# Gate/up projections of four feed-forward blocks by one level of Strassen

## The chip, the cores and the metric

The kernel runs on one core of a Trainium2 chip. The metric is the device time of one execution in microseconds (us). The engines are named as the profile names them: PE is TensorE (PEld its weight loads), DVE VectorE, ACT ScalarE, POOL GpSimd, and SP the engine that here only asks for transfers.

## The reference

A decoder trunk of two layers on 512 tokens of 1024 features, in float32. Each layer is a half-step feed-forward block (FFN), a mixer, and another half-step FFN; layer 0 mixes by attention, layer 1 by an S5 state space.

```python
def swiglu(h, w_gate, w_up, w_down):
    return (jax.nn.silu(h @ w_gate) * (h @ w_up)) @ w_down

for i in range(DEPTH):                       # DEPTH = 2
    x = x + 0.5 * swiglu(rmsnorm(x, ffn1_norm[i]), ffn1_gate[i], ffn1_up[i], ffn1_down[i])
    h = rmsnorm(x, mix_norm[i])
    x = x + mixer(h)                         # attention for i = 0, S5 for i = 1
    x = x + 0.5 * swiglu(rmsnorm(x, ffn2_norm[i]), ffn2_gate[i], ffn2_up[i], ffn2_down[i])
```

The hidden width is 2816, 22 tiles of 128. So there are four FFNs, FFN0 to FFN3, with attention after FFN0 and S5 after FFN2.

## The kernel before

The state `x` lies in SBUF with the features on the partitions: 8 feature tiles of 128 x 512 tokens. Every float32 product is made of three float32r passes (`mm3`, L135 to L139): each operand is split into a high part, rounded to float32r, and a low part, the rest; high x high, high x low and low x high are added up in PSUM.

Weights come through the class `Stream` in the order in which PE reads them: 1 MB loads on SP (L49), up to four in SBUF, the high part by an ACT cast (`wh`, L77) and the low part by a DVE subtraction (`wl`, L79), for 1024 columns at a time and up to three such splits ahead. `ahead` runs after each matmul group.

An FFN goes through its 22 hidden tiles. For each it has two groups of 24 matmuls of 128x128 weights by 512 tokens (`ps_gu`: gate, then up); `post` (L269 to L280) then scales both by `R` (1/rms of each token), takes the swish of the gate on ACT (L272), multiplies (L275) and splits the product into `ah` (ACT, L277) and `al` (DVE, L279). After 6, 12, 17 and 22 tiles the down projection of those tiles follows, for 8 output tiles (`ps_d`), and `upd` (L315) adds half of it to `x`. At the last of them `nxt(d)` starts the next stage's operands for feature tile `d`: `norm_split` makes `xh` on ACT (L195) and `xl` on DVE (L196), and `norm_sum` adds the squares (L203 to L208).

Tables for attention and S5 are made beside the FFNs as background work: `tick(k, rate)` takes steps of generators in `k.bg` after each matmul group until they have used about `rate` microseconds of DVE, by a formula in `Counted`; the rate is 2.0 in FFN0 and 1.4 in FFN1 and FFN2. Every engine takes its instructions in the order written; nothing reorders them.

Of the kernel before, what the change touches and what calls it, by code (L numbers as in the profile page):

```python
# [15 lines left out]
P = 128  # L16
W = 516                                  # columns of a shared working tile
GROUPS = [(0, 6), (6, 6), (12, 5), (17, 5)]
HALF_PI = (1.5703125, 4.837512969970703125e-4, 7.549789948768648e-8)
LN2 = (0.693359375, -2.12194440e-4)  # L20
MAGIC = 12582912.0                       # 1.5 * 2**23: rounds to an integer when added


class Stream:
    """Weights in the order the tensor engine reads them: 1 MB loads, then the exact
    split into a float32r high part (ScalarE) and low part (VectorE)."""

    RAW = 4

    def __init__(self, nc, raw, hl, ahead_load=3, ahead_split=3):  # L30
        self.nc, self.raw, self.hl = nc, raw, hl
        self.AL, self.AS = ahead_load, ahead_split
        self.units, self.gr = [], []
        self.nl = self.ns = self.cur = self.done = 0
        self.rt, self.wt = {}, {}

    def add(self, ap, ncols, grs, split=True):
        u = len(self.units)
        self.units.append((ap, ncols))
        for a, b in grs:  # L40
            self.gr.append((u, a, b, split))

    def load(self, pieces=((0, 2048),)):
        ap, n = self.units[self.nl]
        t = self.raw.tile([P, 2048], F32, tag="raw", name="raw")
        self.rt[self.nl] = t
        self.nl += 1
        for a, b in pieces:
            self.nc.sync.dma_start(t[:, a:min(b, n)], ap[:, a:min(b, n)])  # L49
            yield  # L50

    def load_to(self, u, force=False):
        while self.nl <= min(u, len(self.units) - 1):
            if not force and self.nl - self.RAW >= self.done:
                break
            for _ in self.load():
                pass

    def split_to(self, g, pieces=None, later=None):
        while self.ns <= min(g, len(self.gr) - 1):  # L60
            u, a, b, sp = self.gr[self.ns]
            self.load_to(u, True)
            r = self.rt[u]
            if sp == "pairs":
                h = self.hl.tile([P, 1024], F32R, tag="wh", name="wh")
                z = h[:, :2 * (b - a)].rearrange("p (k two c) -> p k two c", two=2, c=8)
                v = r[:, a:b].rearrange("p (k c) -> p k c", c=8)
                self.nc.scalar.copy(z[:, :, 0], v)
                self.nc.vector.tensor_tensor(z[:, :, 1], v, z[:, :, 0].bitcast(F32), ALU.subtract)
                self.wt[self.ns] = (h, None)  # L70
                self.done = u + 1
            elif sp:
                h = self.hl.tile([P, 1024], F32R, tag="wh", name="wh")
                lo = self.hl.tile([P, 1024], F32R, tag="wl", name="wl")
                for c0, c1 in pieces or ((0, b - a),):
                    rest = (lo[:, c0:c1], r[:, a + c0:a + c1], h[:, c0:c1].bitcast(F32), ALU.subtract)
                    self.nc.scalar.copy(h[:, c0:c1], r[:, a + c0:a + c1])  # L77
                    if later is None:
                        self.nc.vector.tensor_tensor(*rest)  # L79
                    else:  # L80
                        later.append(rest)
                self.wt[self.ns] = (h, lo)
                if self.ns + 1 == len(self.gr) or self.gr[self.ns + 1][0] != u:
                    self.done = u + 1
            else:
                self.wt[self.ns] = (r[:, a:b], None)
            self.ns += 1

    def next(self):
        g = self.cur  # L90
        self.cur += 1
        if g and not self.gr[g - 1][3]:
            self.done = self.gr[g - 1][0] + 1
        self.split_to(g)
        return self.wt.pop(g)

    def finish(self):
        """the units taken so far are read by no later instruction"""
        self.done = self.gr[self.cur - 1][0] + 1

    def ahead(self, later=None):
        """the next splits and loads; VectorE's half of the splits is left to the caller if asked"""
        g = self.cur
        if g < len(self.gr):
            e = min(g + self.AS, len(self.gr) - 1)
            while not self.gr[e][3] and e > g:
                e -= 1
            if self.gr[e][3]:
                self.split_to(e, later=later)
            self.load_to(self.gr[e][0] + self.AL)  # L110


class Counted:
    """VectorE calls of background work, with their length added up."""
# [20 lines left out]
def mm3(nc, ps, wh, wl, xh, xl, start, stop):  # L135
    """one float32 block product in three float32r passes"""
# [5 lines left out]
def rsqrt_steps(k, V, v, n, scale, eps):  # L142
    """v [P, n] sums; yields between steps, last the tile with 1/sqrt(v*scale + eps)"""
# [28 lines left out]
def tick(k, us):  # L172
    """background work worth about `us` of VectorE"""
# [14 lines left out]
# ---------------------------------------------------------------- norms  # L188
def norm_split(k, d, ni):
    """the split of x*g of a feature tile"""  # L190
    if d == 0:
        k.xh = k.big.tile([P, 8, 512], F32R, tag="big", name="xh")
        k.xl = k.big.tile([P, 8, 512], F32R, tag="big", name="xl")
# [4 lines left out]

def norm_sum(k, d):
    """sums of squares"""  # L200
# [28 lines left out]
def stats2(k):  # L229
    """the same, [128 equal rows, 512 tokens]"""  # L230
# [7 lines left out]
# ---------------------------------------------------------------- feed-forward  # L238
def ffn_order():
    o, done = [], 0  # L240
    for gi, (s, n) in enumerate(GROUPS):
        upto = s + n + (0 if gi == len(GROUPS) - 1 else 1)
        while done < upto:
            o.append(("gu", done))
            done += 1
        o.append(("d", gi))
    return o


def ffn_units(st, wgu, wd6, wd5):  # L250
    for kind, i in ffn_order():
        if kind == "gu":
            st.add(wgu[i], 2048, [(0, 1024), (1024, 2048)])
        else:
            n = GROUPS[i][1]
            for j in range(4):
                ap = wd6[i * 4 + j] if i < 2 else wd5[(i - 2) * 4 + j]
                st.add(ap, 2 * n * 128, [(0, n * 128), (n * 128, 2 * n * 128)])


def ffn(k, nxt, rate=0.0, sums=None):
# [3 lines left out]
    act = {}  # L265
    wait = []

    def post():
        m, gp, up = wait.pop(0)  # L269
        g1 = k.G("g1")[:, :512]  # L270
        V.tensor_tensor(g1, gp, k.R, ALU.mult)  # L271
        S.activation(g1, g1, AF.Silu)  # L272
        u1 = k.G("u1")[:, :512]
        V.tensor_tensor(u1, up, k.R, ALU.mult)  # L274
        V.tensor_tensor(u1, g1, u1, ALU.mult)  # L275
        ah = k.G("ah", F32R)[:, :512]
        S.copy(ah, u1)  # L277
        al = k.G("al", F32R)[:, :512]
        V.tensor_tensor(al, u1, ah.bitcast(F32), ALU.subtract)  # L279
        act[m] = (ah, al)  # L280

    for kind, i in ffn_order():
        if kind == "gu":
            ps = []
            for h in range(2):
                w, lo = st.next()
                p = k.PS("ps_gu")
                for kk in range(8):
                    c = slice(kk * 128, kk * 128 + 128)
                    mm3(nc, p, w[:, c], lo[:, c], k.xh[:, kk], k.xl[:, kk], kk == 0, kk == 7)  # L290
                ps.append(p)
                st.ahead()
                if sums and st.AS == 2:
                    run_out(sums)
                    st.AS = 3
                g = 2 * i + h - (1 if sums else 0)
                if g == 1:
                    stats1(k)
                elif g == 2:
                    stats2(k)  # L300
# [1351 lines left out]
```

## Time and profile before

| | |
|---|---|
| Time, median of 3 runs | 1940.06 us (1938.75 to 1940.76) |
| Span of the profiled execution | 1938.9 us |
| Stages: start 0 to 20; FFN0 to 420; attention to 640; FFN1 to 1020; FFN2 to 1400; S5 to 1560; FFN3 to the end | us, rounded |

The span is that of one profiled execution, and everything below is read from it; it lies 1.2 us under the median. A busy share counts the time that an engine works on instructions. Matmuls are pipelined: each is shown longer (0.39 us) than the distance from one start to the next, which is what one costs. "Idle before" and "waits" name the instruction that let a waiting engine go on.

### The profile page before, as it was taken

The numbers are of one execution on the slowest core, as the hardware profiler recorded it, in microseconds if no ns is written. First come the engines' busy times: TensorE is split into PE (matmuls) and PEld (weight loads), VectorE is DVE, ScalarE is ACT, GpSimd is POOL, SyncE is SP. The second block draws the span as 40 slices with busy tenths as digits, with TensorE's granted clock in tenths as the row PEclk, the third lists the DMA queues.
The fourth block names the chain that finished last, engine by engine and source line by source line (L and its number), as shares of the span: only waits on it lengthen the run. The fifth ranks groups of instructions, "written<-read, shape, count | busy, mean of one in ns | idle before, by whom it ended". The sixth has DMA issues, their size and how long they took to land.

```text
span 1938.9 us, 22606 instructions
## 1 busy us (share of the span) xinstructions
PE 1927.5 (99%) x8740; PEld 1560.2 (80%) x8740; DVE 1129.0 (58%) x2153; ACT 672.4 (35%) x1104; POOL 100.6 (5%) x183
## 2 busy tenths in 40 slices
PE   9999999999999999999999999999999999999999
PEld 6788888877788888888888888888888888888887
DVE  6787676557685665456457556444484644444443
ACT  5222222434557432322324322322463432222221
POOL 0000111000011000100100100100000000000000
PEclk9999999999999999999999999999999999999999
DMA  6222334234122323433423443433486322222221
GB/s 246 102 103 97 127 106 134 88 109 125 52 84 56 118 88 125 152 101 108 171 93 129 132 141 104 143 124 106 154 260 208 131 95 80 103 88 97 71 98 44
DMA packets 62780, 227.40 MB, mean 117 GB/s; under 512 B 23744, under 2 KB 23872, under 8 KB 46672
## 3 DMA queue, kind: packets, MB, share of 16 engines
q1 hardware_dynamic: 42736, 192.47, 28.9%
q0 software_dynamic: 11472, 31.36, 5.3%
q10 hardware_dynamic: 8464, 2.12, 0.5%
q8 instruction: 69, 1.13, 0.2%
q14 instruction: 39, 0.32, 0.1%
HBM read 196.17 MB, written 26.61 MB: 115 GB/s over the span
## 4 chain that ended last, share of the span: by engine, by line
PE 96%; DMA 1%; ACT 1%; DVE 1%; issue 1%; SPq 0%; DVEq 0%; ACTq 0%
PE ps_gu L137 17%; PE ps_gu L139 17%; PE ps_gu L138 17%; PE ps_d L138 8%; PE ps_d L139 8%; PE ps_d L137 8%; PE ps_p L421 2%; PE ps_p L423 2%; PE ps_p L422 2%; PE ps_g L137 2%; PE ps_g L138 2%; PE ps_g L139 2%; PE ps_s L1173 1%; PE ps_w L137 1%; PE ps_w L138 1%; PE ps_w L139 1%
## 5 line engine op out<-in xcount | busy, mean ns | idle before, releaser
L137 PE MATMUL ps_gu<-xh,wh 128*128 128x512 f32 x1408 | 561.4, 399 | 2.8 <-ACT xh L195 2.8
L139 PE MATMUL ps_gu<-xh,wl 128*128 128x512 f32 x1408 | 557.7, 396 | 0.0
L138 PE MATMUL ps_gu<-xl,wh 128*128 128x512 f32 x1408 | 555.9, 395 | 0.2 <-DVE xl L196 0.2
L77 ACT CAST wh<-raw 128x1024 fp32r<-128x1024 f32 (+3 forms) x354 | 334.1, 947 | 518.6 <-PE ps_d L138 250.4
L79 DVE TENSOR_TENSOR wl<-raw,wh 128x1024 fp32r<-128x1024 f32 (+3 forms) x235 | 260.3, 1110 | 174.4 <-ACT wh L77 172.7
L137 PEld LDWEIGHTS ps_gu<-xh,wh 128*128 128x128 f32 x1408 | 265.0, 188 | 66.7 <-ACT xh L195 3.1
L139 PEld LDWEIGHTS ps_gu<-xh,wl 128*128 128x128 f32 x1408 | 264.9, 188 | 65.2
L138 PEld LDWEIGHTS ps_gu<-xl,wh 128*128 128x128 f32 x1408 | 265.0, 188 | 64.5 <-DVE xl L196 1.1
L137 PE MATMUL ps_d<-ah,wh 128*128 128x512 f32 x704 | 277.9, 395 | 0.0
L138 PE MATMUL ps_d<-al,wh 128*128 128x512 f32 x704 | 277.4, 394 | 0.0
L139 PE MATMUL ps_d<-ah,wl 128*128 128x512 f32 x704 | 277.3, 394 | 0.0
L315 DVE SCALAR_TENSOR_TENSOR x<-ps_d,x 128x512 f32<-128x512 f32 x128 | 88.5, 691 | 193.0 <-PE ps_d L139 192.7
L274 DVE TENSOR_TENSOR u<-ps_gu,R 128x512 f32<-128x512 f32 x88 | 60.8, 691 | 194.7 <-PE ps_gu L139 194.7
L137 PEld LDWEIGHTS ps_d<-ah,wh 128*128 128x128 f32 x704 | 132.2, 188 | 30.8
L139 PEld LDWEIGHTS ps_d<-ah,wl 128*128 128x128 f32 x704 | 132.2, 188 | 30.8
L138 PEld LDWEIGHTS ps_d<-al,wh 128*128 128x128 f32 x704 | 132.3, 188 | 30.6
L277 ACT CAST ah<-u 128x512 fp32r<-128x512 f32 x88 | 54.7, 622 | 267.4 <-DVE u L275 265.0
L272 ACT ACTIVATE g<-g 128x512 f32<-128x512 f32 x88 | 55.7, 633 | 206.4 <-DVE g L271 206.4
L318 DVE TENSOR_TENSOR wl<-raw,wh 128x1024 fp32r<-128x1024 f32 (+2 forms) x101 | 104.7, 1036 | 0.3 <-ACT wh L77 0.3
L279 DVE TENSOR_TENSOR al<-u,ah 128x512 fp32r<-128x512 f32 x88 | 61.0, 693 | 60.5 <-ACT ah L277 60.5
L421 PE MATMUL ps_p<-wh,xh 128*128 128x512 f32 x192 | 79.0, 411 | 0.0
L423 PE MATMUL ps_p<-wh,xl 128*128 128x512 f32 x192 | 76.0, 396 | 0.0
(298 smaller groups left out, 1939.1 us busy)
## 6 DMA issues: line engine op xcount, KB each, us to landing
raw<-in_wgu SPq DMA_DIRECT2D x87, 1024.0 KB, 4.8
raw<-in_wd SPq DMA_DIRECT2D x32, 768.0 KB, 4.4
raw<-in_wd SPq DMA_DIRECT2D x32, 640.0 KB, 3.9
raw<-in_wq SPq DMA_DIRECT2D x12, 1024.0 KB, 4.8
raw<-in_wglu SPq DMA_DIRECT2D x8, 1024.0 KB, 4.9
raw<-in_wo SPq DMA_DIRECT2D x4, 1024.0 KB, 4.8
dW<-t POOLq DMA_DIRECT2D x16, 256.0 KB, 2.5
dY<-y POOLq DMA_DIRECT2D x16, 256.0 KB, 3.3
```

Source lines behind the costliest of these rows:

```text
L77: self.nc.scalar.copy(h[:, c0:c1], r[:, a + c0:a + c1])
L79: self.nc.vector.tensor_tensor(*rest)
L137: nc.tensor.matmul(ps, wh, xh, start=start, stop=False)
L138: nc.tensor.matmul(ps, wh, xl, start=False, stop=False)
L139: nc.tensor.matmul(ps, wl, xh, start=False, stop=stop)
L272: S.activation(g1, g1, AF.Silu)
L274: V.tensor_tensor(u1, up, k.R, ALU.mult)
L279: V.tensor_tensor(al, u1, ah.bitcast(F32), ALU.subtract)
L315: V.scalar_tensor_tensor(k.x[:, d], p, 0.5, k.x[:, d], ALU.mult, ALU.add)
L318: V.tensor_tensor(*a)
L421: T.matmul(ps[t], xh, w[:, c], start=kk == 0, stop=False)
L423: T.matmul(ps[t], xl, w[:, c], start=False, stop=kk == 7)
```

## The change

Gate and up projections are done for pairs of hidden tiles (`NPAIR = 11` per FFN). The weights of a pair are cut in four by the halves of the hidden tile pair and of the features (a11, a12, a21, a22), the normalised input in four by features and tokens. One level of Strassen's method makes the product of two such 2x2 arrangements from seven half-size products, P1 to P7, instead of eight, with sums of weight blocks, sums of input blocks and sums of results.

- **Products.** `prod` issues 24 matmuls of 256 tokens: 4 pairs of feature tiles x gate and up x 3 passes. `ffn_plan` sets the order P1, P4 of the pair before, P2, P5, P6, P3, P7. The first pair of an FFN interleaves P1, P2 and P5 (`first`). Down projections follow every second pair, with three pairs in the last group. The down projection's matmuls are the same in number and size.
- **Weight sums.** Units are of 512 KB, up to eight in SBUF. P5 needs a21 + a22 and P7 needs a11 + a21: the second block is added to the first while it is loaded, by a DMA on the POOL queue (`flush`). For P6 and P3 DVE adds another unit to P5's (`then`). Seven splits of 1024 columns per pair replace four, up to two ahead.
- **Input sums.** `forms` makes the seven sums of input blocks for each pair of feature tiles and splits each into `Fh` and `Fl`; for FFN0 its additions are on POOL, elsewhere on DVE.
- **Result sums.** P1, P5 and the sum called U2 are copied from PSUM by ACT (`hold`); c11, c12, c21 and c22 are put together from PSUM and these copies on DVE. A queue (`after`, `slot`) delays each by a step.
- **Around it.** Background work is doled at 0.9 (FFN0) and 0.8 (FFN1, FFN2) per product; one S5 table generator moves from FFN0 to FFN1; S5's frames of `x` are loaded at FFN2's end. SBUF buffers are allocated by stage (`k.region`). All comments are dropped.

On DVE in the gate/up stage of FFN2, before, two hidden tiles stand so (`g`, `u` gate and up, `wl` a weight's low part):

```order
L271 TENSOR_TENSOR g_8770<-ps_gu,R 128x512
L274 TENSOR_TENSOR u_8773<-ps_gu,R 128x512
L275 TENSOR_TENSOR u_8773<-g_8770,u_8773 128x512
L279 TENSOR_TENSOR al<-u_8773,ah 128x512
L79 TENSOR_TENSOR wl<-raw,wh 128x1024 x2
```

And after, one pair in FFN3 (`ps_f` a product in PSUM, `P_`, `U_` copies of others, `raw<-raw` a weight sum):

```order
L422 TENSOR_TENSOR g_15767<-ps_f,U_15869 128x2x256
L423 TENSOR_TENSOR g_15767<-g_15767,R 128x1024
L113 TENSOR_TENSOR wl<-raw,wh 128x1024
L431 TENSOR_TENSOR g_15934<-ps_f,P_15765 128x2x256
L432 TENSOR_TENSOR g_15934<-g_15934,R 128x2x256
L404 TENSOR_TENSOR g_15767<-g_15767 128x512
L113 TENSOR_TENSOR wl<-raw,wh 128x1024
L119 TENSOR_TENSOR raw<-raw 128x1024
L410 TENSOR_TENSOR al<-g_15767,ah 128x512
L113 TENSOR_TENSOR wl<-raw,wh 128x1024
L119 TENSOR_TENSOR raw<-raw 128x1024
L436 TENSOR_TENSOR g_15934<-ps_f,R 128x2x256
```

Splits now stand between the steps of the results, each behind an ACT result that it or the next one needs.

On DVE at the end of attention, before, each feature tile has its update of `x`, its low part and its sum:

```order
L836 TENSOR_TENSOR x<-x,ps_w 128x512
L196 SCALAR_TENSOR_TENSOR xl<-x,cst,xh 128x512
L127 TENSOR_TENSOR acc<-acc,sq 128x512
L890 TENSOR_TENSOR wl<-raw,wh 128x1024
L79 TENSOR_TENSOR wl<-raw,wh 128x1024
```

After, the last two feature tiles there (`fa`, `fb` input sums):

```order
L1039 TENSOR_TENSOR x<-x,ps_w 128x512
L250 TENSOR_TENSOR fa<-fa 128x256
L263 TENSOR_TENSOR Fl<-fa,Fh 128x2x256
L165 TENSOR_TENSOR acc<-acc,sq 128x512
L1039 TENSOR_TENSOR x<-x,ps_w 128x512
L255 TENSOR_TENSOR fb<-fb,fa 128x256
L256 TENSOR_TENSOR fa<-fa,fb 128x256
L258 TENSOR_TENSOR fa<-fa,fb 128x256
L263 TENSOR_TENSOR Fl<-fb,Fh 128x4x256
L263 TENSOR_TENSOR Fl<-fa,Fh 128x256
L165 TENSOR_TENSOR acc<-acc,sq 128x512
L1094 TENSOR_TENSOR wl<-raw,wh 128x1024
```

The last low part of FFN1's first weights stands behind all of them.

On POOL at the start of the program, after (before, these rows are absent and loads for the background work follow the fills at once):

```order
L1748 MEMSET zz 128x256
L1749 MEMSET maskw 128x135
L1750 MEMSET maskw 128x16
L250 ISA
L250 TENSOR_TENSOR fa<-fa 128x256
L255 TENSOR_TENSOR fb<-fb,fa 128x256
L256 TENSOR_TENSOR fa<-fa,fb 128x256
L258 TENSOR_TENSOR fa<-fa,fb 128x256
L75 DMA raw<-in_wgu 128x1024
L250 TENSOR_TENSOR fa<-fa 128x256
```

An accumulating load stands between the sums of the first two feature tiles and those of the next.

The core of the diff:

```diff
+    def flush(self):
+        for t, ap in self.accs:
+            self.nc.gpsimd.dma_start(t, ap, accum_op=ALU.add)
...
+                if then is not None:
+                    ops.append((r[:, :n], r[:, :n], self.rt[then][:, :n], ALU.add))
...
+def forms(k, d, ni, E=None):
...
+    xd, g, kp = k.x[:, d].rearrange("p (t c) -> p t c", t=2), k.C("vec")[:, ni * 8 + d:ni * 8 + d + 1], d // 2
+    if d % 2 == 0:
+        a = k.fa = k.GU("fa")
+        S.activation(a[:, 0:3:2], xd, AF.Identity, scale=g)
+        E.tensor_tensor(a[:, 1], a[:, 0], a[:, 2], ALU.subtract)
+        parts = ((0, 2, a[:, 0:2]),)
+    else:
+        a, b = k.fa, k.GU("fb")
+        S.activation(b[:, 0:2], xd, AF.Identity, scale=g)
+        E.tensor_tensor(b[:, 3], b[:, 1], a[:, 2], ALU.subtract)
+        E.tensor_tensor(a[:, 1], a[:, 1], b[:, 1], ALU.add)
+        S.activation(b[:, 2], a[:, 1], AF.Copy, scale=-1.0)
+        E.tensor_tensor(a[:, 3], a[:, 1], b[:, 0], ALU.subtract)
+        parts = ((2, 6, b), (6, 7, a[:, 3:4]))
+    for s, e, v in parts:
+        h = k.Fh[:, s:e, kp]
+        S.copy(h, v)
+        V.tensor_tensor(k.Fl[:, s:e, kp], v, h.bitcast(F32), ALU.subtract)
...
+    o = [("first", 0), ("P6", 0), ("P3", 0), ("P7", 0)]
+    for j in range(1, NPAIR):
+        o += [("P1", j), ("P4", j - 1), ("P2", j), ("P5", j), ("P6", j), ("P3", j), ("P7", j)]
...
+    def prod(ps, wl, s, start, kps=range(4)):
+        w, lo = wl
+        for kp in kps:
+            for h in range(2):
+                c = slice(h * 512 + kp * 128, h * 512 + kp * 128 + 128)
+                o, xh, xl = ps[:, h * 256:h * 256 + 256], k.Fh[:, s, kp], k.Fl[:, s, kp]
+                first = start and kp == 0 and h == 0
+                for i, (a, b) in enumerate(((w, xh), (w, xl), (lo, xh))):
+                    nc.tensor.matmul(o, a[:, c], b, start=first and i == 0, stop=kp == 3 and i == 2,
+                                     skip_group_check=True)
...
+        after(1, {"P1": lambda: hold("P1", ps), "P2": lambda: c11(j), "P5": lambda: hold("P5", ps),
+                  "P6": lambda: hold("U2", ps), "P3": lambda: c12(j), "P7": lambda: c22(j),
+                  "P4": lambda: c21(j)}[kind])
```

## Rows read from the trace of the kernel before

**Rows 1.** Busy time, share of the span and instructions of each engine.

```profile
PE 1927.5 (99%) x8740; PEld 1560.2 (80%) x8740; DVE 1129.0 (58%) x2153; ACT 672.4 (35%) x1104; POOL 100.6 (5%) x183
```

**Rows 2.** The chain that ended last, share of the span by line.

```profile
PE 96%; DMA 1%; ACT 1%; DVE 1%; issue 1%; SPq 0%; DVEq 0%; ACTq 0%
PE ps_gu L137 17%; PE ps_gu L139 17%; PE ps_gu L138 17%; PE ps_d L138 8%; PE ps_d L139 8%; PE ps_d L137 8%; PE ps_p L421 2%; PE ps_p L423 2%; PE ps_p L422 2%; PE ps_g L137 2%; PE ps_g L138 2%; PE ps_g L139 2%; PE ps_s L1173 1%; PE ps_w L137 1%; PE ps_w L138 1%; PE ps_w L139 1%
```

**Rows 3.** PE's waits: in total, times, longest (us).

```profile
PE ps_gu L137 <- ACT xh L195: 2.8, 1, 2.8
...
PE ps_gu L138 <- DVE xl L196: 0.2, 1, 0.2
```

**Rows 4.** Timeline of PE, steady down projection: start, length (us).

```profile
99.81 0.39 PE L137 MATMUL ps_d<-ah,wh 128*128 128x512 f32 x1
...
101.44 0.39 PE L138 MATMUL ps_d<-al,wh 128*128 128x512 f32 x1
```

**Rows 5.** Instructions by line: busy us, mean ns, idle before.

```profile
L137 PE MATMUL ps_gu<-xh,wh 128*128 128x512 f32 x1408 | 561.4, 399 | 2.8 <-ACT xh L195 2.8
...
L277 ACT CAST ah<-u 128x512 fp32r<-128x512 f32 x88 | 54.7, 622 | 267.4 <-DVE u L275 265.0
L272 ACT ACTIVATE g<-g 128x512 f32<-128x512 f32 x88 | 55.7, 633 | 206.4 <-DVE g L271 206.4
```

**Rows 6.** Timeline of PE in attention, L780 and what follows.

```profile
575.50 0.29 PE L780 MATMUL ps_s<-fb 68*128 68x256 f32 x1
575.62 0.60 PE L460 MATMUL ps_t<-cst,qr 128*128 128x128 f32 x4
...
577.48 0.40 PE L780 MATMUL ps_s<-fb 68*128 68x512 f32 x1
577.72 0.40 PE L137 MATMUL ps_w<-oh,wh 128*128 128x512 f32 x1
```

**Rows 7.** Timeline in S5: matmuls of 64 columns.

```profile
1421.91 4.35 PE L1282 MATMUL ps_S<-U,raw 128*128 128x64 f32 x38
1421.91 4.21 PEld L1282 LDWEIGHTS ps_S<-U,raw 128*128 128x128 f32 x37
```

**Rows 8.** Timeline of DVE at the end of FFN1.

```profile
1026.39 0.69 DVE L127 TENSOR_TENSOR acc<-acc,sq 128x512 f32<-128x512 f32 x1
1026.99 0.68 DVE L315 SCALAR_TENSOR_TENSOR x<-ps_d,x 128x512 f32<-128x512 f32 x1
1027.59 1.22 DVE L318 TENSOR_TENSOR wl<-raw,wh 128x1024 fp32r<-128x1024 f32 x1
1028.72 0.75 DVE L196 SCALAR_TENSOR_TENSOR xl<-x,cst,xh 128x512 fp32r<-128x512 f32 x1
```

**Rows 9.** Timeline of the start.

```profile
0.74 0.31 POOL L1517 MEMSET zz<- 128x256 f32 x1 [0.29 <-POOLq L1643]
...
4.22 0.72 ACT L195 ACTIVATE xh<-x,cst 128x512 fp32r<-128x512 f32 x1 [2.20 <-DMA cst<-in_cst]
...
5.29 0.50 PE L137 MATMUL ps_gu<-xh,wh 128*128 128x512 f32 x1
...
9.45 0.79 PE L137 MATMUL ps_gu<-xh,wh 128*128 128x512 f32 x1 [2.83 <-ACT xh L195]
...
17.03 2.01 ACT L77 CAST wh<-raw 128x1024 fp32r<-128x1024 f32 x2 [0.81 <-DMA raw<-in_wgu]
```

**Rows 10.** DVE's waits for ACT: in total, times, longest (us).

```profile
DVE wl L79 <- ACT wh L77: 172.7, 128, 8.6
DVE al L279 <- ACT ah L277: 60.5, 88, 0.7
```

**Rows 11.** Stretches: length, busy of each engine, clock, DMA share, GB/s.

```profile
0.00:20.00 20.00, 15.74 (x45) 9.77 (x46) 12.18 (x20) 13.54 (x22) 1.41 (x8) 0.83 0.91 340
1400.00:1560.00 160.00, 158.81 (x860) 134.78 (x859) 102.61 (x158) 76.34 (x110) 0.00 (x0) 0.95 0.59 197
```

**Rows 12.** DMA issues: times, KB each, median us to landing.

```profile
raw<-in_wgu SPq DMA_DIRECT2D x87, 1024.0 KB, 4.8
...
dW<-t POOLq DMA_DIRECT2D x16, 256.0 KB, 2.5
```

More of the change, by code (lines that the diff above doesn't have):

```diff
@@ L24, with __init__, unit, entry @@
 class Stream:
[L28 to L45, printed above, removed]
+    RAW = 8
+    def __init__(self, nc, raw, hl, ahead=2):
+        self.nc, self.raw, self.hl, self.AS = nc, raw, hl, ahead
+        self.units, self.ents, self.refs = [], [], []
+        self.nl = self.ns = self.cur = self.live = 0
+        self.rt, self.wt, self.accs, self.open = {}, {}, [], []
+        self.ready = lambda: True
+    def unit(self, ncols, ap, more=None, late=False):
+        self.units.append((ap, ncols, more, late))
+        self.refs.append(0)
+        return len(self.units) - 1
+    def entry(self, u, split=True, then=None, pool=None):
+        self.ents.append((u, split, then, pool))
+        self.refs[u] += 1
+        if then is not None:
+            self.refs[then] += 1
+    def add(self, ap, ncols, split=True, late=False, pool=None):
+        self.entry(self.unit(ncols, ap, late=late), split, pool=pool)
+    def unref(self, u):
+        self.refs[u] -= 1
+        if not self.refs[u]:
+            self.live -= 1
+    def load(self, pieces=((0, 1024),)):
+        ap, n, more, _ = self.units[self.nl]
+        t = self.raw.tile([P, 1024], F32, tag="raw", name="raw")
         self.rt[self.nl] = t
         self.nl += 1
+        self.live += 1
+        self.flush()
         for a, b in pieces:
@@ L50, in load, with fill @@
             yield
-    def load_to(self, u, force=False):
-        while self.nl <= min(u, len(self.units) - 1):
-            if not force and self.nl - self.RAW >= self.done:
+        if more is not None:
+            self.accs.append((t[:, :n], more))
+    def flush(self):
+        for t, ap in self.accs:
+            self.nc.gpsimd.dma_start(t, ap, accum_op=ALU.add)
+        self.accs = []
+    def fill(self, upto=None, force=False):
+        n = len(self.units) if upto is None else upto + 1
+        while self.nl < n:
+            if not force and (self.live >= self.RAW or self.units[self.nl][3] and not self.ready()):
                 break
+            assert self.live < self.RAW
             for _ in self.load():
@@ L59, in split_to @@
     def split_to(self, g, pieces=None, later=None):
[L60 to L63, printed above, removed]
-            if sp == "pairs":
[L65 to L69, printed above, removed]
+        V, S = self.nc.vector, self.nc.scalar
@@ new lines, in split_to @@
+        while self.ns <= min(g, len(self.ents) - 1):
+            u, sp, then, pool = self.ents[self.ns]
+            self.fill(u, True)
+            if self.accs:
+                self.flush()
+            r, n = self.rt[u], self.units[u][1]
+            hl = pool() if pool else self.hl
+            if sp == "pairs":
+                h = hl.tile([P, 1024], F32R, tag="wh", name="wh")
+                z = h[:, :2 * n].rearrange("p (k two c) -> p k two c", two=2, c=8)
+                v = r[:, :n].rearrange("p (k c) -> p k c", c=8)
+                S.copy(z[:, :, 0], v)
+                V.tensor_tensor(z[:, :, 1], v, z[:, :, 0].bitcast(F32), ALU.subtract)
@@ L70, in split_to @@
                 self.wt[self.ns] = (h, None)
-                self.done = u + 1
+                self.unref(u)
             elif sp:
[L73 to L77, printed above, removed]
-                    if later is None:
-                        self.nc.vector.tensor_tensor(*rest)
+                h = hl.tile([P, 1024], F32R, tag="wh", name="wh")
@@ new lines, in split_to @@
+                lo = hl.tile([P, 1024], F32R, tag="wl", name="wl")
+                ops = []
+                for c0, c1 in pieces or ((0, n),):
+                    S.copy(h[:, c0:c1], r[:, c0:c1])
+                    ops.append((lo[:, c0:c1], r[:, c0:c1], h[:, c0:c1].bitcast(F32), ALU.subtract))
+                    if later is None:
+                        V.tensor_tensor(*ops.pop())
+                if then is not None:
+                    ops.append((r[:, :n], r[:, :n], self.rt[then][:, :n], ALU.add))
+                    self.unref(then)
@@ L97, in finish, with ahead @@
     def finish(self):
[L99 to L110, printed above, removed]
+        for u in self.open:
+            self.unref(u)
+        self.open = []
+    def ahead(self, later=None, n=None):
+        e = min(self.cur + (self.AS if n is None else n), len(self.ents) - 1)
+        while e >= self.cur and not (self.ents[e][1] and self.ents[e][3] is None):
+            e -= 1
+        if e >= self.ns:
+            self.split_to(e, later=later)
+        self.fill()
 class Counted:
@@ new lines, with ffn_plan, ffn_units, unit @@
+SLOT = {"P1": 0, "P2": 2, "P5": 1, "P6": 4, "P3": 3, "P7": 5, "P4": 6}
+def ffn_plan():
+    o = [("first", 0), ("P6", 0), ("P3", 0), ("P7", 0)]
+    g = 0
+    for j in range(1, NPAIR):
+        o += [("P1", j), ("P4", j - 1), ("P2", j), ("P5", j), ("P6", j), ("P3", j), ("P7", j)]
+        if g < len(GROUPS) - 1 and j == GROUPS[g][0] + GROUPS[g][1]:
+            o.append(("d", g))
+            g += 1
+    return o + [("d0", g), ("P4", NPAIR - 1), ("d", g)]
+def ffn_units(st, wgu, wd4, wd6):
+    U = {}
+    def unit(kind, j):
+        if (kind, j) not in U:
+            a11, a12, a21, a22 = [wgu[j, q] for q in range(4)]
+            U[kind, j] = st.unit(1024, *{"P1": (a11,), "P2": (a12,), "P4": (a22,), "P5": (a21, a22),
+                                         "P7": (a11, a21)}[kind])
+        return U[kind, j]
+    for kind, j in ffn_plan():
+        if kind == "first":
+            for q in ("P1", "P2"):
+                st.entry(unit(q, j))
+            kind = "P5"
+        if kind == "P5":
+            st.entry(unit("P5", j), then=unit("P1", j))
+        elif kind == "P6":
+            st.entry(unit("P5", j), then=unit("P2", j))
+        elif kind == "P3":
+            st.entry(unit("P5", j))
+        elif kind == "d0":
+            st.add(wd6[0], 768)
+        elif kind == "d" and j == len(GROUPS) - 1:
+            for d in range(1, 8):
+                st.add(wd6[d], 768)
+        elif kind == "d":
+            for q in range(4):
+                st.add(wd4[j, q], 1024)
+        else:
+            st.entry(unit(kind, j))
@@ L361, in attn_units @@
         for j in range(2):
-            st.add(wo[hf, j], 2048, [(0, 1024), (1024, 2048)])
+            for h in range(2):
+                st.add(wo[hf, j][:, h * 1024:h * 1024 + 1024], 1024)
 def attn_setup(k, rel):
@@ L906, in s5_units, with glu @@
     st = k.st
[L907 removed]
+    def glu(m, pool=None):
+        for h in range(2):
+            st.add(wglu[m][:, h * 1024:h * 1024 + 1024], 1024, pool=None if h else pool)
     glu(0)
     glu(1)
[L910 to L913 removed]
+    for o in range(8):
+        st.add(k.dW[o], 1024, split=False, late=True)
+    for o in range(8):
+        st.add(k.dT[o], 1024, split=False, late=True)
+        st.add(k.dY[o], 1024, split=False, late=True)
+    glu(2, lambda: k.reg["hls"])
+    for m in range(3, 8):
         glu(m)
@@ L927, in s5_tables @@
     tw = G("s5tm")
-    step, mag, th, c, s, a, b, cr = [tw[:, i * 64:i * 64 + 64] for i in range(8)]
+    step, mag, th, a, b, cr = [tw[:, i * 64:i * 64 + 64] for i in range(6)]
+    c, s = k.cs[:, :64], k.cs[:, 64:]
     ci = k.lj
```

444 lines of the change are left out of this document (259 added, 185 removed).

## The prediction

> **What bounds the kernel now.** I read the busy shares first [rows 1]: TensorE is busy 99% of the span, VectorE 58%, ScalarE 35%. The chain that ended last is TensorE for 96%, and the three gate/up lines hold 17% each of it [rows 2]. TensorE's waits name six entries that add up to 7.5 us; the largest is 2.8 us at the start [rows 3]. So TensorE never starves, and time can be saved only by giving it less. In steady matmuls of 512 columns, seven starts lie between 99.81 and 101.44 us [rows 4]: 0.2329 us each. Gate/up issues 3 x 1408 = 4224 of them [rows 5], 984 us.
>
> **Removed and added on TensorE.** Seven products for eight turn 4224 matmuls of 512 columns into 44 pairs x 7 x 24 = 7392 of 256 columns. That is half the columns and 14 for 8 in number, so all rests on a 256-column matmul with a fresh weight block each time. The trace has a few: L780 with 256 columns starts at 575.50 and the next matmul at 575.62; with 512 columns 577.48 and 577.72 [rows 6]. So 0.12 us. Lower bound: 38 matmuls of 64 columns, bound by their weight loads, take 4.35 us with the last one's drain, and their 37 loads 4.21, 0.114 each [rows 7]. Upper bound: 512 columns at 2.4 GHz are 213 ns, the rows have 233, and 20 ns more on 107 ns are 0.127. I take 0.120: 7392 x 0.120 = 887 us. Term: 887 - 984 = **-97** (from -141 at 0.114 to -45 at 0.127).
>
> **What VectorE gets.** Durations: start to start, 1024 columns take 1.13 us (1027.59 to 1028.72), 512 take 0.60 (1026.39 to 1026.99) [rows 8]; halved again, 256 columns about 0.34. Before, two hidden tiles cost VectorE 4 splits x 1.13 + 8 operations x 0.61 = 9.4 us beside 96 x 0.2329 = 22.4 us of TensorE. After, a pair costs 7 splits and 2 weight sums and the scaling of 1024 columns (10 x 1.13 = 11.3) and nine of 512 (5.5): 16.8 us, beside 168 x 0.120 = 20.2. ScalarE gets 7 casts at 1.0 (two take 2.01 [rows 9]) and 7 operations at about 0.52 start to start (0.62 long [rows 5]): 10.7. All still fit. But background work (the bias and S5 tables) is doled at 0.9 or 0.8 per step, so about 6.0 us per pair more while it lasts: 22.8 for 20.2.
>
> The two engines also wait for each other, in queues that run in order. Three times a pair a VectorE result goes to ScalarE (swish, 0.63 [rows 5]), behind which stands the cast (1.0) that VectorE's next split needs. VectorE does this already: `al` waits for `ah` 88 times, 60.5 us, and splits for casts 172.7 us in 128 waits [rows 10]; there TensorE's lead covers it. Three times 1.65 are 5.0, so 21.8 us per pair without background work. With it some of the wait is filled; I take 2.2 left, 25.0 per pair (bounds 22.8 to 27.8). Against that stands a lead of two products, 2 x 24 x 0.12 = 5.8 us, made good at each down projection (96 matmuls, 22.3 us, for some 13 us of VectorE), once per two pairs. So two pairs stall TensorE 2 x (25.0 - 20.2) - 5.8 = 3.8 us with background work and nothing without; and the copy of P5 out of PSUM, which stands on ScalarE behind `ah` of the tile before, is about 1 us late at P3 in both. Two pairs: 5 us or 1. FFN0 has background work in about half its 5.5 two-pair stretches, FFN1 in all, FFN2 in two thirds, FFN3 in none: 15 + 25 + 19 + 5 = **+64** (bounds 5 to 105).
>
> **The start.** Now the first two matmul groups start at 5.29 and 9.45 us [rows 9], and the mean granted clock of the first 20 us is 0.83 [rows 11]: a good part of them runs at the lower level, 1.2 GHz. After, the operand sums of the first features are on the POOL queue, and behind the first four stands the accumulating load of P5, which waits for P5's plain load. By then SP has asked for 4.1 MB; at the 340 GB/s of this stretch [rows 11] they are here at 12 us, plus 2 for the tail of a transfer: 14. Only then follow the sums of the other three feature pairs, each a ping-pong of six ScalarE steps (0.72, 0.62, 0.72, 0.4, 1.0, 0.4) and POOL steps between: 5.2 us. The casts of P2 and P5 stand behind all of them on ScalarE: 14 + 3 x 5.2 = 30, first full product at 31, where before 512-column matmuls ran from 9.45. TensorE's work done by then is a few matmuls in both, and the half-clock stretch comes again after the idle time: **+20**. A tensor operation on POOL isn't in the trace; the nearest row is a 256-column fill, 0.31 us [rows 9]. With that price the ping-pong is 4 us and the term 14; with 1 us each it is 28.
>
> The Trainium skill ("SBUF — State Buffer", section "Who interferes with whom") says that a VectorE instruction with two SBUF inputs contends with a GpSimd instruction that reads SBUF. No row here has both at once; by it the start would lie nearer its upper end.
>
> **The stages' ends.** At the end of attention a pair of features now takes, in line through both engines: x 0.6, gain 0.7, subtract 0.34, add 0.34, negate 0.4, add 0.34, cast 1.0, low part 1.13, low part 0.34, sum of squares 0.6; and for its first half x, gain, subtract, cast, low part, sum: 3.9. About 9.8 us, with TensorE giving it 24 matmuls, 5.6 us. Before it was x 0.60, xl 0.7 and the sum 0.60 [rows 8] per feature, under 5. Four pairs fall behind by 4.2 each, 17; and P5's low weights stand behind the last form on VectorE, 3 more: **+20** (10 to 28). At FFN1's end 18 matmuls per feature leave 8.4 us a pair, so the lag is 1.4 a pair, the down weights' splits come late (4), and P5's low part is again behind the last form (about 6): **+15** (5 to 22).
>
> **Smaller.** After `first`, P6's cast stands behind the copies of P1 and P5 (0.62 after the last matmul, then 1.0, then 1.13 of low part): 2.8 x 4 = **+11** (4 to 14). Half-clock stretches after such stops **+3** (0 to 10; the S5 stretch shows a mean granted clock of 0.95 [rows 11]). S5's frames load beside FFN2's tail, **+3** (0 to 10).
>
> The 86 accumulating loads add 0.5 MB each, the traffic 44 x 1.5 MB. They are asked for some seven products, 20 us, early; a 1 MB load lands in 4.8 us, POOL's 256 KB in 2.5 [rows 12]. 150 GB/s stands against 340 seen at the start. I take 0 (upper end 40: every accumulation late by half a microsecond).
>
> **Sum.** -97 + 64 + 20 + 20 + 15 + 11 + 3 + 3 = +39. On the profiled execution's 1938.9 us: 1978; the median of the runs lies 1.2 above that execution, so **1979 us**.
>
> **Rivals.**
> *A. The lag stays hidden* (the other side: faster). For it: VectorE is only 84% loaded without background work, 16.8 of 20.2, and now waits for ScalarE without TensorE noticing [rows 3, 10]. Against it: with background work it has no room at all. It decides where a pair with background work costs VectorE and ScalarE under about 23.1 us (2 x 2.9 = 5.8 of lead). Then 5 stays of the 64: 1938.9 - 97 + 5 + 72 = 1919, and with start and ends at their lower bounds (33 for 72) 1880. 1880 to 1925.
> *B. Accumulating loads are late.* POOL's queue also carries background DMAs that wait for VectorE; an accumulation behind one of these is late and with it P5 and P7. At +40: 2019 and up. Against it the 20 us of lead.
> *C. Weight loads are not hidden.* If a 256-column matmul waited for its weight load, each would take 0.114 + 0.107 = 0.22 us: 7392 x 0.22 = 1626, +642, about 2620 with the rest. The 0.12 us between starts [rows 6] and the 0.2329 at 512 columns [rows 4] speak against it.
> The Trainium skill ("TensorE: Matmul & The Clock Gate", section "The mechanism") says that weight loads overlap running matmuls only where the row groups differ; all here use 128 rows. The rows contradict it, hence the small chance.
> *D. The product count is not what decides:* gate/up is paced by VectorE, and the price of the matmul hardly matters: at 0.114 the stalls grow by what TensorE gains, 1.0 us per pair, 44 in all. This only narrows the forecast.
>
> **Numbers.** Forecast 0.62 (its own range 1945 to 2010), A 0.27, B 0.09, C 0.02. About 0.2% (4 us) is what a measurement of this kernel can tell from no change. Slower: 0.57 of the forecast, all of B and C: 0.68. Faster: 0.25 of A and 0.03 of the forecast: 0.28. Same: 0.02 of each, 0.04. The range leaves out C, the upper half of B and the low end of A: 1895 to 2030.
>
> **What would show it.** The spacing of the 256-column matmuls: 0.12 us. TensorE busy near 93% of the span, with waits on the low weights (VectorE) and on the copies of P1 and P5 (ScalarE) some 60 us in all, mostly in FFN1 and least in FFN3. First full product at about 31 us. A gap of some 20 us before FFN1 and of 15 before FFN2. VectorE busy about 1129 + 44 x 7.4 + 25 = 1480 us. Wrong would be a TensorE at 98% in the gate/up stages (A), waits for transfers there (B), or spacing above 0.13 (C).

## The result, and the profile after

The changed kernel takes 2087.2 us (median; 2081.25 to 2089.69) where the kernel before takes 1939.56 in the same comparison: a ratio of 1.0755, 95% interval [1.0738, 1.0772]. It is slower, as forecast, but by 148 us and not by 39, and the time lies outside the range of 1895 to 2030.

Busy time of the changed kernel, share of the span and instructions of each engine, beside [rows 1]:

```profile
PE 1880.4 (90%) x11908; PEld 1689.6 (81%) x11908; DVE 1494.6 (72%) x2525; ACT 891.2 (43%) x1400; POOL 189.8 (9%) x287
```

And the chain that ended last, by engine, beside [rows 2]:

```profile
PE 61%; DVE 22%; ACT 7%; issue 5%; DMA 4%; POOL 1%; SPq 0%; ACTq 0%; DVEq 0%; POOLq 0%
```

TensorE worked 47 us less, but held 96% of the chain before and holds 61% now. A third of the chain is VectorE, ScalarE and the handing over between them. Its waits (total, times, longest), beside the 7.5 us of [rows 3]:

```profile
PE ps_f L393 <- ACT wh L110: 49.7, 10, 23.8
PE ps_f L393 <- ACT P L398: 42.2, 22, 4.0
PE ps_f L393 <- DVE g L431: 38.0, 16, 5.0
PE ps_s L1391 <- DVE e L165: 30.0, 10, 5.6
```

The first line is mostly the start (30.8 us of it lie in FFN0). The next two are the repeated ones: a product waits until ScalarE has copied the previous content of its PSUM bank (L398) or VectorE has read it (L431). The last is background work's own matmuls, which stand in TensorE's queue and wait for VectorE.

The price of a matmul came out at or below the forecast. Starts of 256-column matmuls, twelve apart, in FFN0 and in FFN3 (timeline of TensorE; start, length in us):

```profile
43.83 0.29 PE L393 MATMUL ps_f<-Fl,wh 128*128 128x256 f32 x1
...
45.25 0.28 PE L393 MATMUL ps_f<-Fl,wh 128*128 128x256 f32 x1
```

```profile
1820.00 0.28 PE L393 MATMUL ps_f<-Fl,wh 128*128 128x256 f32 x1
...
1821.36 0.28 PE L393 MATMUL ps_f<-Fl,wh 128*128 128x256 f32 x1
```

1.42 us for 12 are 0.118 us each, 1.36 are 0.113. Both spacings run through the whole kernel; the mean of all starts less than 0.13 us apart is 0.115. What decides between the two stays open. So the rest is gaps. The next table is worked out from the starts of all matmuls: the stage's length from its first product to its last matmul; what its gate/up and down matmuls take at the upper spacing, 0.1177, and at 0.2328 us; what the distance between two starts is above that at half the clock (up to 0.2135 and 0.427); and what is left, TensorE idle. Background matmuls make up the rest.

| stage | before, us | after, us | after: matmuls | half clock | idle |
|---|---|---|---|---|---|
| TensorE's first matmul (1.2) to the first product | 4.1 | 9.8 | | | |
| FFN0 | 380.0 | 421.2 | 340.4 | 18.6 | 56.8 |
| attention | 272.2 | 273.5 | | | |
| FFN1 | 379.3 | 443.5 | 340.4 | 21.1 | 70.3 |
| FFN2 | 375.7 | 412.5 | 340.4 | 12.5 | 46.9 |
| S5 | 152.0 | 162.1 | | | |
| FFN3 | 370.0 | 359.7 | 340.4 | 2.6 | 13.7 |

Before, the matmuls of an FFN take 368.7. Each FFN saves 28.3 us of TensorE at the upper spacing; at the mean of 0.115 it is 33, and the waits are 5 us per FFN larger than the table has them. The same reckoning of the kernel before leaves 11 us of half clock and idle in all four. FFN3, which has no background work beside it, keeps 10 of them. The other three lose them and 37 to 64 us more.

### The profile page after: what moved, and what is told of

Read it like the earlier page. It is cut to its first block, busy times and chain, and to the rows that moved or that the text cites. A ratio compares the mean times of both kernels' runs of the same rounds, so it can differ in the third digit from the quotient of the medians.

```text
span 2087.9 us, 30415 instructions
## 1 busy us (share of the span) xinstructions
PE 1880.4 (90%) x11908; PEld 1689.6 (81%) x11908; DVE 1494.6 (72%) x2525; ACT 891.2 (43%) x1400; POOL 189.8 (9%) x287
## 3 DMA queue, kind: packets, MB, share of 16 engines
q1 hardware_dynamic: 71392, 215.55, 30.7%
q0 software_dynamic: 24144, 77.50, 17.5%
## 4 chain that ended last, share of the span: by engine, by line
PE 61%; DVE 22%; ACT 7%; issue 5%; DMA 4%; POOL 1%; SPq 0%; ACTq 0%; DVEq 0%; POOLq 0%
PE ps_f L393 24%; PE ps_d L177 7%; PE ps_d L175 7%; PE ps_d L176 7%; DVE wl L113 6%; ACT wh L110 4%; DVE raw L119 2%; PE ps_p L624 2%; PE ps_p L626 2%; PE ps_p L625 2%; PE ps_g L175 1%; PE ps_g L176 1%; PE ps_g L177 1%; DVE g L404 1%; PE ps_y L1557 1%
## 5 line engine op out<-in xcount | busy, mean ns | idle before, releaser
L393 PE MATMUL ps_f<-Fh,wh 128*128 128x256 f32 x2464 | 721.0, 293 | 137.1 <-ACT wh L110 49.7
L393 PE MATMUL ps_f<-Fh,wl 128*128 128x256 f32 x2464 | 711.2, 289 | 18.8 <-DVE wl L528 6.1
L393 PE MATMUL ps_f<-Fl,wh 128*128 128x256 f32 x2464 | 710.2, 288 | 0.0
L393 PEld LDWEIGHTS ps_f<-Fh,wh 128*128 128x128 f32 x2464 | 491.6, 199 | 152.0 <-ACT wh L110 56.8
L113 DVE TENSOR_TENSOR wl<-raw,wh 128x1024 fp32r<-128x1024 f32 (+2 forms) x362 | 434.7, 1204 | 217.7 <-ACT wh L110 217.4
L110 ACT CAST wh<-raw 128x1024 fp32r<-128x1024 f32 (+2 forms) x454 | 456.6, 1027 | 270.7 <-PE ps_d L176 167.3
L393 PEld LDWEIGHTS ps_f<-Fh,wl 128*128 128x128 f32 x2464 | 489.5, 199 | 21.7 <-DVE wl L113 6.8
L393 PEld LDWEIGHTS ps_f<-Fl,wh 128*128 128x128 f32 x2464 | 490.4, 199 | 1.1 <-DVE Fl L263 0.2
L119 DVE TENSOR_TENSOR raw<-raw 128x1024 f32<-128x1024 f32 x86 | 105.4, 1225 | 2.9
L488 DVE TENSOR_TENSOR wl<-raw,wh 128x1024 fp32r<-128x1024 f32 x64 | 77.8, 1216 | 13.6 <-ACT wh L110 13.6
L398 ACT COPY P<-ps_f 128x512 f32<-128x512 f32 x88 | 50.7, 577 | 59.1 <-PE ps_f L393 59.1
```

Source lines behind the costliest of these rows:

```text
L110: S.copy(h[:, c0:c1], r[:, c0:c1])
L113: V.tensor_tensor(*ops.pop())
L119: V.tensor_tensor(*o)
L393: nc.tensor.matmul(o, a[:, c], b, start=first and i == 0, stop=kp == 3 and i == 2, skip_group_check=True)
L488: tt(*a)
```

## The experiments

The question was what makes TensorE wait in FFN0 to FFN2. Theory 1: VectorE and ScalarE together set the pace once background work is added. Rival 2: the order of the products and the PSUM copies do, whatever else VectorE has to do. Rival 3: accumulating loads come late. What is compared is a cycle of FFN1: two pairs of hidden tiles and one down projection, from one down projection's first matmul to the next one's, the mean of four. With no waits it is 2 x 168 x 0.118 + 96 x 0.2329 = 62.0 us (61.0 at 0.115).

**No background work beside the FFNs.**

```diff
-            ffn(k, nt(1), 0.9, sums, ...
+            ffn(k, nt(1), 0.0, sums, ...
-            ffn(k, ft(3), 0.8)
+            ffn(k, ft(3), 0.0)
```

(and the third likewise)

> No background work beside the FFNs (all three rates 0); it is done in one piece behind FFN0 and at FFN2's end, so the total says little and the stages are read. Theory 1 (VectorE with ScalarE paces the gate/up stage once background work is added to 16.8 us per pair): two pairs of FFN1 fall from about 73 us to the 63.6 of FFN3, FFN1 from 443.5 to about 390, its half-clock time from 21 to under 8 us. Rival 2 (the order of the products and the PSUM copies make TensorE wait whatever else VectorE does): two pairs stay above 70, FFN1 above 430. Rival 3 (accumulating loads come late): FFN1 unchanged.

Four cycles of FFN1 of the changed kernel (length, then busy time of PE, PEld, DVE, ACT and POOL, granted clock, DMA share, GB/s):

```profile
808.48:1105.35 296.87, 267.97 (x1787) 248.71 (x1785) 240.96 (x435) 109.98 (x174) 53.99 (x80) 0.94 0.57 164
```

And of this one:

```profile
812.35:1066.41 254.06, 247.29 (x1730) 229.29 (x1729) 180.43 (x200) 103.03 (x129) 12.82 (x15) 1.00 0.52 146
```

A cycle falls from 74.2 to 63.5 us, FFN1 from 443.5 to 389.8, its half-clock time from 21.1 to 6.3 us. The order of products is the same in both, so rivals 2 and 3 by themselves explain at most the 1.5 us above 62.0 (2.5 above 61.0). In the changed kernel VectorE is busy 60.2 us of each 74.2 and idle for 14. What it waits for there:

```profile
DVE wl L113 <- ACT wh L110: 28.1, 19, 1.6
DVE x L470 <- PE ps_d L177: 13.1, 14, 2.1
DVE wl L488 <- ACT wh L110: 7.0, 2, 6.6
```

35 us in four cycles are casts, waited for in a queue that can't go on to other work; 13.1 are the down projection's results. And what TensorE waits for in the same four cycles:

```profile
PE ps_s L1391 <- DVE e L165: 12.6, 4, 5.6
PE ps_f L393 <- DVE g L431: 10.1, 4, 4.0
PE ps_f L393 <- ACT P L398: 4.1, 3, 2.7
PE ps_s L1391 <- ACT U L398: 2.1, 1, 2.1
```

None of it is a weight's split. (The view names gaps over 0.15 us.) 14.2 us are products that wait until a PSUM bank is read or copied; without background work these are 6.8. The other 14.7 are background matmuls (L1391) that stand in TensorE's queue and hold up the products behind them; without background work there are none. So the run takes away two things at once, VectorE's load and these matmuls, and no run tried them apart. All of the loss lies beside the gate/up products. The four stretches of two pairs, then the four down projections, in the same columns:

```profile
sum 207.07, PE 178.17 PEld 175.98 DVE 176.70 ACT 84.86 POOL 36.38; mean PE 44.54 PEld 43.99 DVE 44.17 ACT 21.21 POOL 9.10
```

```profile
sum 89.80, PE 89.80 PEld 72.73 DVE 64.26 ACT 25.12 POOL 17.61; mean PE 22.45 PEld 18.18 DVE 16.07 ACT 6.28 POOL 4.40
```

A pair takes 25.9 us, a down projection 22.4, as long as its matmuls need. (The total of this kernel, 2236 us, includes the background work done in one piece, and says nothing.)

**No weight sums on VectorE.**

```diff
-                if then is not None:
-                    ops.append((r[:, :n], r[:, :n], self.rt[then][:, :n], ALU.add))
```

(only the addition goes; the unit's bookkeeping stays)

> Leaves out VectorE's two weight sums per pair (P6 and P3 are then made with P5's weights), 2 x 1.13 = 2.3 us of VectorE per pair and nothing else. Theory 1 (VectorE with ScalarE paces): two pairs of FFN1 fall by about 4.5 us from 73, FFN1 by about 25, FFN2 by 15 to 25; FFN3 (22.1 us per pair) by up to 2 per pair, since TensorE's own work is 19.8. Rival 2 (the order of the products makes TensorE wait): under 8 us in FFN1.

```profile
772.70:1050.97 278.27, 259.86 (x1786) 241.09 (x1785) 222.20 (x420) 110.01 (x174) 54.57 (x80) 0.97 0.61 176
```

VectorE is busy 4.7 us less per cycle, and the cycle is 4.6 us shorter (69.6). FFN1 falls by 26.5, FFN0 by 27, FFN2 by 22, FFN3 by 14, the kernel to 1995 us. In FFN1 all of what VectorE saves comes out as time, and the background matmuls' waits fall with it, from 14.7 to 8.4 us in four cycles. In FFN3, without background work, 14 of some 26 us do (a quarter of the 105.4 us that VectorE spends on these sums in the changed kernel).

**Half the rate.**

```diff
-            ffn(k, ft(3), 0.8)
+            ffn(k, ft(3), 0.4)
```

(and 0.45 and 0.4 in FFN0 and FFN2)

> Background work at half its rate per step in all FFNs (what is left is done in one piece at FFN2's end, so the stages are read, not the total). Theory 1: a cycle of two pairs in FFN1, 74 us at the full rate and 63.5 without any, comes out near the middle, 67 to 70. If background work only hurts when it passes a threshold (VectorE has room to spare before TensorE starves), it stays below 65.5.

```profile
785.43:1056.53 271.10, 253.91 (x1742) 235.06 (x1741) 221.69 (x419) 104.14 (x138) 39.39 (x53) 0.97 0.59 159
```

67.8 us per cycle. VectorE's busy time is 55.4 us per cycle, 10.3 above none and 4.8 below the full rate: steps of the background generators are larger than 0.4 us by the formula of `Counted` (0.60 for 512 columns), so this is two thirds rather than half. These 10.3 cost 4.3 us, the next 4.8 cost 6.4. The first part is partly hidden. The last costs more than itself: the waits of background matmuls in TensorE's queue rise with it from 2.2 to 14.7 us in four cycles, 3.1 per cycle. (The total, 2092 us, again has what is left done in one piece.) A clean threshold at TensorE's 62 us there is not.

**Splits three products ahead.**

```diff
-    def __init__(self, nc, raw, hl, ahead=2):
+    def __init__(self, nc, raw, hl, ahead=3):
-    RAW = 8
+    RAW = 6
-    rawp, hl = E(name="rawp", bufs=Stream.RAW), E(name="hl", bufs=4)
+    rawp, hl = E(name="rawp", bufs=Stream.RAW), E(name="hl", bufs=5)
```

> Splits three products ahead instead of two (five split buffers for four; six weight units in SBUF for eight). The prediction counted the lead of two products as 5.8 us that each down projection makes good. If that holds, one product more saves about 2.9 us per two pairs in FFN1, 16 in all. If VectorE and ScalarE are behind on the average of a whole cycle (61.6 us of VectorE work and some 11 of waits in 73), a longer lead is used up once: FFN1 within 4 us of 443.5.

```profile
804.58:1098.28 293.70, 262.47 (x1786) 243.19 (x1785) 241.49 (x437) 110.37 (x174) 55.09 (x81) 0.95 0.59 167
```

FFN1 falls by 20 us, which at first looks like the first reading. But the four cycles fall by 3.2 us in all (73.4 each). The rest is at FFN1's seams: from its first product to the 72nd matmul after it 24.6 us for 33.6, from the last down projection's start to the end 37.2 for 43.8. A longer lead helps where this stage begins, and does nearly nothing for the pace. FFN0 gets 6 us longer, FFN2 6 shorter. The total is 2068 us. Six weight units for eight came with the edit, and what they cost was not tried apart.

**No accumulating loads.**

```diff
         if more is not None:
-            self.accs.append((t[:, :n], more))
+            pass
```

> Leaves out all 88 accumulating loads (P5 and P7 are then made without a22 and a21). Theory 1: the accumulating loads cost nothing in the steady stage, FFN1 and FFN3 as after (443.5 and 359.7, within 3); only the start gets about 6 us shorter, since GpSimd's sums no longer wait for P5's load. Rival 3 (accumulating loads come late): FFN1 at least 20 shorter.

FFN1 442.9 and FFN3 357.6: rival 3 is out. FFN0 is 9.8 us shorter; 3.9 of it at the start, where the long stop ends at 33.98 us for 37.85. The total is 2072 us.

**Idle matmuls in the gaps.**

```diff
         w = st.next()
+        if fill and kind == "P4":
+            keep_busy(k, 10)
```

(`fill` for FFN1 alone)

> Ten idle matmuls of 512 columns in bf16 (2.2 us) ahead of every P4 of FFN1, 110 in all, 24 us of TensorE. Theory 1: TensorE has 70 us of idle time in FFN1, so FFN1 is no longer (443.5 within 5). If the half-clock stretches (21 us in FFN1) cost time of their own, the filler keeps the clock up and FFN1 gets shorter by 5 to 20. If TensorE itself is the pace (rival 2 in its extreme form): 24 longer.

FFN1 takes 444.2 us for 443.5, with 24 us more work on TensorE. Its idle time falls from 70.3 to 54.4 and its half-clock time from 21.1 to 13.8; the total is 2087 us as before the edit. So most of the half-clock time in FFN1 lies in time that TensorE would have waited anyway; it isn't a cost to be added to the waits.

**The start, sums on VectorE.**

```diff
-                forms(k, d, 0, nc.gpsimd)
+                forms(k, d, 0)
```

> Operand sums of the start on VectorE instead of GpSimd. If the start is long because the accumulating load stands in front of the sums on GpSimd's queue: the stop that ends at 37.85 us ends at about 22 (the weight sum for P5 lands near 20), total 15 us less. If only GpSimd's slowness (0.72 us for 256 columns) counts: 16 additions x 0.4 = 6 us less. If the late arrival of P5's weights decides: no change.

Total 2069.7, 17.5 us less; but the stop ends at 29.48, 8.4 us earlier, and not at 22. FFN0 ends 12.1 us earlier; the rest lies in later stages, which the edit doesn't touch. What stood there in the changed kernel (timeline of the start):

```profile
5.43 0.72 POOL L250 TENSOR_TENSOR fa<-fa 128x256 f32<-128x256 f32 x1 [4.05 <-ACT fa L249]
...
16.05 1.00 POOL L75 DMA_DIRECT2D raw<-in_wgu  x1 [6.35 <-DMA raw<-in_wgu]
```

```profile
36.75 1.99 ACT L110 CAST wh<-raw 128x1024 fp32r<-128x1024 f32 x2
...
37.85 0.58 PE L393 MATMUL ps_f<-Fh,wh 128*128 128x256 f32 x1 [23.84 <-ACT wh L110]
```

The accumulating load is asked for at 16.05, and three rounds of sums of 7.2 us follow. On VectorE a round takes 6.1 us, from one operand to the next through ScalarE, and nothing waits for the load; but four rounds in line, with the casts of P2 and P5 behind them, still end near 28. Each of the three readings was partly wrong: the chain of rounds itself is most of the stop.

**Seven products in FFN3 alone.** FFN0 to FFN2 get eight products in the new stream:

```diff
+    def tile(j, q):
+        w, lo = st.next()
+        i, kh = q // 2, q % 2
+        ...
+                mm3(nc, T["ps"][h], w[:, c], lo[:, c], k.xh[:, 2 * kp + kh], k.xl[:, 2 * kp + kh], ...)
```

> Eight products as before in FFN0 to FFN2 (in the new weight units of 512 KB, no weight sums), seven in FFN3 alone, which has no background work. Theory 1: FFN0 to FFN2 take 380, 379 and 376 us again and FFN3 about 360 for 370: total 1929 to 1940. If the new stream, memory regions or S5's loads cost time of their own, FFN0 to FFN2 come out above 385 each and the total above 1950.

1953.43 us, ratio 1.0062 [1.0047, 1.0077]. FFN3 takes 361 us, 9 less than before; the start 6.5 more; S5 164.7 for 152.0. Four variants then went after the start and S5.

> The variant with seven products in FFN3 alone, and two edits: at the start the second unit's cast stands in front of the last four operand splits (FFN0's first stops of 3.7 and 1.4 us go, about 5 us); in S5 two idle bf16 matmuls ahead of each of the 16 groups of 64-column products (0.43 us each, 3.5 us in the first eight). If the half-clock stretch of S5 (37 us here, 17 before) comes from short gaps and narrow matmuls, it gets shorter and S5 with it by 3 to 8; if not, S5 gets 5 longer. Total 1940 to 1955.

1948.95 us. The start is as before again (FFN0 ends 1 us earlier than before). The idle matmuls in S5 did not help: 166.0 us, 34 of them at half clock.

> Seven products in FFN3 alone, with the start of h2, without its idle matmuls; splits three products ahead with six units in SBUF; and the last two of S5's four frame loads (1 MB) asked for behind the last load of U. In h1 VectorE waited 4.1 and 3.8 us at S5's start for U, whose loads stand behind the frames and weight units on SP's queue. If that wait and the longer half-clock stretch behind it make S5 162 us instead of 152, S5 comes back to 152 to 156 and the total to 1932 to 1940. If the frames are not the reason, S5 stays above 160 and the total above 1943.

1940.01 us, ratio 1.0002 [0.9993, 1.0011]. VectorE's waits for U fall from 7.9 to 2.2 us and FFN3 to 357.7, but S5 stays at 163.1.

> As h3, but seven weight units in SBUF (29 small working tiles for 31), and S5's last two frames asked for behind the weight units. In h3 S5 took 163 us for 152: its first products wait 3.4 us for a unit, and TensorE then runs at half its clock for 37.5 us (17.1 before). If that stop brings the clock down earlier, S5 comes to 152 to 157 and the total to 1928 to 1934. If the clock falls anyhow, S5 stays above 160 and the total within 3 us of h3's 1940.

1939.61 us, ratio 0.9990 [0.9981, 0.9999]; S5 159.7, FFN3 362.8.

> As h4 with eight units, 31 working tiles and splits two products ahead: FFN3 361 instead of 358. S5 as in h4, by the same two readings; total 3 us above h4.

1938.82 us, ratio 0.9991 [0.9976, 1.0007]; S5 158.7, FFN3 359.8. The stretch of S5 in the kernel before, and in the next to last variant:

```profile
1412.90:1564.80 151.90, 150.71 (x824) 128.30 (x823) 95.08 (x147) 65.97 (x98) 0.00 (x0) 0.94 0.57 190
```

```profile
1411.30:1571.00 159.70, 158.64 (x823) 136.49 (x824) 103.74 (x165) 72.88 (x110) 1.78 (x2) 0.89 0.59 190
```

TensorE is busy all through in both; it works at a lower mean clock (0.94 and 0.89). The half-clock stretch lasts 17.1 us before and 30.7 to 37.5 in the variants. It sets in 32.8 us into S5 before, and between 21.9 and 27.5 in the variants, each time near a gap of 1.0 to 4.2 us among the 64-column matmuls. Less half of that stretch, S5 takes 143.4 us before and 142.6 to 145.9 in the four variants without idle matmuls there: nearly all of the difference goes with the clock. The wait for U is not the reason: in the last variant it is 0.5 us, as before, and S5 takes 158.7. Why the stretch lasts longer stays open. So what FFN3 gains S5 nearly gives back: no median of these beats the kernel before by more than 0.1%.

## Why the prediction was wrong

- **Removed and added on TensorE.** Right in kind, too small in size: 0.115 us on the mean for a 256-column matmul (0.120 taken), 7392 x 0.115 - 984 = -134 for -97. With this price its own sum would have come out at +2, unless stalls grow by what TensorE gains, as its rival D has it. So that the direction was right is in part luck: an overpriced matmul stood in for waits that were not seen. Rival C (0.22 us) is out.
- **The start, +20.** Too low: matmuls run one after another from 37.85 us, where before they did from 9.45, 28.4 later and at the upper end of its 14 to 28. An addition on GpSimd takes 0.72 us, where the nearest row was a fill of 0.31; a round takes 7.2 us instead of 5.2. (At 0.31 its own steps add up to 5.1, not to the 4 that it names.)
- **The stages' ends, +20 and +15.** Right, in place and size. Stops at FFN1's and FFN2's first products:

```profile
711.76 0.58 PE L393 MATMUL ps_f<-Fh,wh 128*128 128x256 f32 x1 [5.21 <-ACT wh L110]
713.35 0.58 PE L393 MATMUL ps_f<-Fh,wl 128*128 128x256 f32 x1 [0.80 <-DVE wl L1090]
721.73 0.58 PE L393 MATMUL ps_f<-Fh,wh 128*128 128x256 f32 x1 [7.16 <-ACT wh L110]
728.59 0.58 PE L393 MATMUL ps_f<-Fh,wl 128*128 128x256 f32 x1 [6.06 <-DVE wl L1094]
...
1160.70 0.58 PE L393 MATMUL ps_f<-Fh,wl 128*128 128x256 f32 x1 [6.07 <-DVE wl L528]
```

  The first four are 19.2 us. At FFN2's begin, with the stops of 3.2, 1.4, 0.9 and 1.7 ahead of the last row, it is 13.3. P6's lateness is 2.9 us in FFN0 and 2.4 in FFN3 (2.8 forecast); in the other two it is part of the stops above. All these stops, the start's 25 among them, are 63 us; 66 were forecast.
- **What VectorE gets, +64.** Here it failed. Idle and half-clock time in the FFNs are 243 us (last two columns of the table); without the 63 of the seams, 180 are left, where the prediction had 64 and 3 for the clock. (It counts 5 stretches of two pairs per FFN where it names 5.5; its own figures give 70.) Without background work it was right: 63.7 us per cycle forecast, 63.5 measured, in FFN3 too. With it, it forecast 67.5 and 74.2 were measured. The step that failed is "Against that stands a lead of two products, 2 x 24 x 0.12 = 5.8 us, made good at each down projection". The stretch of two pairs takes 51.8 us: about twice the 25.0 that it put on a pair, and not the 44.2 that the lead would leave.

  Why the lead gave nothing: it is a lead of split weights, and TensorE waited for none of these in the four cycles. It waited 14.2 us for PSUM banks, which VectorE and ScalarE read and copy between the splits made ahead, and 14.7 for background's own matmuls, a path that the prediction doesn't have. Nor is the down projection a time to catch up: `tick` hands out background work there too (L489), VectorE is busy 16.1 us where 13 were counted (12.9 without), and in the 6.4 that remain it waits for casts and for that projection's results. A lead of three left the cycle at 73.4. How the 12 us lost per cycle divide between VectorE's load and the background matmuls is not shown; that less load on VectorE shortens the cycle one for one is (the run without weight sums).
- **S5, +3.** 10.1 measured. VectorE's waits for U (6.7 us, 0.5 before) were the thing foreseen; but 8.5 of the 10.1 go with a longer half-clock stretch (34.1 us for 17.1), which was not.
- **Rival A** named the point from which the lag shows and held it open; that point rests on the same 5.8 us, and fell with it. B is out by the run without accumulating loads (88, where it counted 86). D is consistent with the idle filler: 24 us of TensorE cost nothing in FFN1. "TensorE busy near 93%" was 90%, "VectorE about 1480 us" was 1494.6. The waits on low weights that it named as a sign are there only at the stages' seams.

## What to carry to other kernels

Arithmetic saved on the bound engine counts only where the next engines have room over a whole cycle, their waits on each other included. Here VectorE's 60.2 us and its 8.8 of waits for casts are 69.0 for TensorE's 62.0, before any lead is counted. (Busy time and all waits together always give the cycle, and show nothing.) A lead covers a beginning, and only a wait for what it holds ready: ask for each engine's wait what ends it. Work that stands in the bound engine's own queue and waits for the loaded one belongs in the sum. Removing background work from the stage, or one instruction per step, shows whether the load counts.

## What the runs showed of the hardware

- A 256-column float32r matmul with new weights of 128 rows and columns each time starts every 0.113 or 0.118 us, 0.115 on the mean, against 0.2329 for 512 columns: splitting the free size in two costs nothing on TensorE, within 1%.
- Ten idle matmuls per pair did keep the clock up more of the time (half-clock time 21.1 to 13.8 us in FFN1, mean granted clock of the four cycles 0.94 to 0.98) and gained nothing. In S5, where TensorE is busy all through, 14 to 20 us more at half clock go with 7 to 14 us more of S5; why the clock stays down longer was not found.
- An accumulating load of 512 KB from GpSimd's queue lands in 6.5 us (median), a plain one in 3.4; with the accumulating loads left out, FFN1 takes 442.9 us for 443.5.
